# Sums of the inputs stored unsplit by GpSimd, split after reloading; the attention's memory pool on the other side; one difference on VectorE

## The chip, the cores and the metric

The kernel runs on one core of one Trainium2 chip. The metric is the device time of one execution in microseconds (us). The engines that matter here are TensorE (PE, matrix multiplications), VectorE (DVE), ScalarE (ACT), GpSimd (POOL) and SyncE (SP). SP does nothing but issue transfers (DMAs), one after the other, in a fixed order; GpSimd has a queue of transfers of its own. All transfers of both queues share the core's 16 DMA engines.

## The reference

One step of a one-layer streaming encoder, for 512 new frames and 32 frames of a running stream, which the kernel treats as one block of T = 544 columns. Cut to what this case touches:

```
h   = layer_norm(x)                                  # 2048 features per frame
proj = h @ w_in                                      # split into hq, hf, hi, hg (8 heads each), cq, ckv, kr
o_h = hgrn2(hq, 1-f, log f, hi, state)               # gated linear recurrence, head by head
q   = rms_norm(cq) @ w_q_b ;  lat = rms_norm(ckv)    # latent attention, 8 heads
k, v = (lat_past ++ lat) @ w_kv_b
o_a = softmax(q k^T + q_rope k_rope^T, chunk mask) v
out = concat(o_h, o_a) @ w_out
h   = layer_norm(ALPHA * h + out)
y   = layer_norm(ALPHA * h + conv_ffn(h))
```

Everything is float32. The outputs are y, the new latents and rope keys, the recurrent states and the last rows of the convolution.

## The kernel before, in words

**Tiles.** Activations lie transposed: 128 features on the partitions, T = 544 columns. `h` is 16 such tiles (k = 0..15), kept as a high and a low half (`aH`, `aL`) so that a float32 product is three passes of TensorE: high by high, low by high weight, high by low weight (`mm3`, L148). `H_` are the two halves of the columns, 272 each. A weight block of 128x1024 is loaded into `raw` (`load_raw`, L127), split into `wh` by ACT (L136) and `wl` by DVE (L137). The unsplit tiles of `h` also lie in DRAM as `h0d`.

**Stages in order of time.** Layer norm of the input, transposes and the `cq` projection; then the attention stage, whose tiles come from the pool `mp` (and `mpr`): projections of `ckv` and `kr`, head 0's q and f (`head_qf(0)`), four pairs of attention heads (`proj_pair`, `attend`) and head 0's i and g (`head_ig(0)`), interleaved by `weave`. Then the divided products for heads 1 to 7 with pools `smr` and `gp`; then the first output piece (`out_first`); then the output projection, the norm and the feed-forward part.

**Divided products.** For heads 1 to 7 a product of 1024 inputs by 2 is made as seven products of half size instead of eight (`divided`, in the order 11, s1, s2, s4, s3, 12, 22; 24 multiplications of 272 columns each, L865). They need four signed sums of the half rows of tile k and tile 8+k, for k = 0..7: s1, s2, s3, s4.

**The sums, before.** `sums_of_inputs` makes them beside the `ckv`, `kr` and `head_qf(0)` products. For each k it loads two rows of `h0d` (L685, L686, 272 KB each, on SP), combines their halves with four DVE operations of 272 columns (L183, L186), splits both results into high (ACT, L697) and low (DVE, L698), and stores the halves with four transfers on SP (L700, 272 KB each). The tiles for the rows are reused (three `p`, two `kn`), and so are the four that hold the split results, so that later loads and splits wait for earlier stores. Later s1 and s2 (L730) come back as already split tiles of 1088 KB, s3 into the freed column halves of `aH` and `aL` (L765), and s4 (L730) into pool `gp`.

**What sets the order.** Each engine runs its instructions in the order in which they were put; SP's list is one queue, so a transfer that waits for something holds all transfers behind it, weights included. `form_next` puts copies of w_out blocks (`wf...`, L93) on SP and accumulating ones on GpSimd at set places. In the divided stage PE, DVE and ACT follow an order written by hand: `turns` says at which slot (half a product) the steps of `levels` (the recurrence's tables, L904 to L946) and `finish` of a head run. `levels(0)` begins at slot 0, before the s1 product.

**The end of the attention stage.** `attend(3)` stores its outputs `o` (`catd`, L670), GpSimd takes the difference of its two heads in place (L671), and SP stores it (`d3d`, L672). The pools of the divided stage overlay the memory of `mp`: `Kp` (L907) lies where `o` lay, so it waits for that last store.

**After the divided stage.** `out_first` multiplies cat tiles, reloaded into `cx` (slots of the old s1, s2 tiles) and split. The next stage loads `h0d` rows into `za` (GpSimd, L1505) and `zb`, adds the output, and takes column sums (L1127). `za` overlays tiles that the last `finish` still stores from (`sm`).

Of the kernel before, what the change touches and what calls it, by code (L numbers as in the profile page):

```python
# [7 lines left out]
F32 = mybir.dt.float32  # L8
# [51 lines left out]
def tile_encoder_step(ctx, tc, xp, xs, w_in, w_in4, w_kr, w_q_b, w_kv_b, w_out, w_out4, w_up, w_gate, w_down, w_down2,  # L60
# [16 lines left out]
    d3_dr = [dram.tile([P, 2, NI], F32, name=f"d3d{k}", tag=f"d3d{k}") for k in range(HK // 2)]  # L77
    si_dr = {n: [dram.tile([P, 2, 4, NI], F32, name=f"si{n}{i}", tag=f"si{n}{i}") for i in range(2)]
             for n in ("s1", "s2", "s3", "s4")}
    sm_dr = [dram.tile([P, 3, 4, NI], F32, name=f"sm{i}", tag=f"sm{i}") for i in range(2)]  # L80
# [320 lines left out]

    with tc.tile_pool(name="mp", bufs=1) as mp, tc.tile_pool(name="psa", bufs=4, space=PSUM) as psa:
        mpr_stack = ExitStack()
        mpr = mpr_stack.enter_context(tc.tile_pool(name="mpr", bufs=1, side="right", reuse_waits="tile"))
        cos = mpr.tile([P, T], F32, name="cos")
# [205 lines left out]
        def attend(pr):  # L611
# [17 lines left out]
            def turn(b, p):  # L629
                tp = a_tile()  # L630
                t = mp.tile([P, 512], F32, name="pT", tag="pT", bufs=3)
                if b == 4:
                    PE.transpose(tp[:, 0:P], p[:, 0:P], ident)
                    PE.transpose(tp[:, P:2 * P], p[:, 32:160], ident)
                    A.activation(plast[96:128, :], tp[96:128, P:P + 64], AF.Copy)
                    n = 64
                else:
                    n = (b + 1) * P
                    for k in range(b + 1):
                        PE.transpose(tp[:, k * P:(k + 1) * P], p[:, k * P:(k + 1) * P], ident)  # L640
                A.activation(t[:, :n], tp[:, :n], AF.Copy)
                return t
# [27 lines left out]
            dma(cat_dr[4 + pr], o)  # L670
            G.tensor_tensor(out=o[:, :, :NI], in0=o[:, :, :NI], in1=o[:, :, NI:], op=ALU.subtract)  # L671
            dma(d3_dr[pr], o[:, :, :NI])  # L672
# [7 lines left out]

        def sums_of_inputs():
            for k in range(HK):
                tag, n, bufs = (("p", T, 3), ("kn", NK, 2))[k % 2]
                a, b = (mp.tile([P, n], F32, name=tag, tag=tag, bufs=bufs)[:, :T] for _ in range(2))
                dma(a, h0_dr[k])  # L685
                dma(b, h0_dr[HK + k])  # L686
                t0, t1, t0b, t1b = (x[:, h] for x in (a, b) for h in H_)
                yield
                minus(t1b, t1b, t1)
                minus(t1, t0, t1)  # L690
                opposite(t0, t1b, t0)
                opposite(t0b, t0, t0b)
                for x, names, (tag, n) in ((a, ("s2", "s3"), (("o", 2 * T), ("qr0", 2 * T))[k % 2]),
                                           (b, ("s4", "s1"), (("vt", 12 * P), ("qr1", 2 * T))[k % 2])):
                    hl = mp.tile([P, n], R, name=tag, tag=tag)[:, :2 * T].rearrange("p (i w c) -> p i w c", i=2, w=2)
                    x2 = x.rearrange("p (w c) -> p w c", w=2)
                    A.activation(hl[:, 0], x2, AF.Copy)  # L697
                    V.tensor_tensor(out=hl[:, 1], in0=x2, in1=hl[:, 0].bitcast(F32), op=ALU.subtract)  # L698
                    for w, name in enumerate(names):
                        dma(si_dr[name][k // 4][:, :, k % 4], hl[:, :, w].bitcast(F32))  # L700
                yield
# [11 lines left out]
        while len(forms) > 24:  # L713
            form_next()
        ropes = [[t[:, j * T:j * T + TP] for j in range(2)]
                 for t in (mp.tile([P, 2 * T], R, name=f"qr{g}", tag=f"qr{g}") for g in range(2))]
        run(proj_pair(0))
# [4 lines left out]
        sr_stack = ExitStack()  # L722
        smr = sr_stack.enter_context(tc.tile_pool(name="smr", bufs=1, side="right", reuse_waits="tile"))
        sums = {}

        def load_sum(p, name):
            sums[name] = [p.tile([P, 8 * NI], R, name=f"{name}{i}", tag=f"{name}{i}").rearrange("p (i k c) -> p i k c", i=2, k=4)
                          for i in range(2)]
            for i in range(2):
                dma(sums[name][i].bitcast(F32), si_dr[name][i])  # L730

        for name in ("s1", "s2"):
            load_sum(smr, name)
        weave([head_ig(0)], [attend(3)], 2.0)

# [12 lines left out]

    with tc.tile_pool(name="gp", bufs=1) as gp, tc.tile_pool(name="psg", bufs=1, space=PSUM) as psg:
        hm = gp.tile([P, T + 272 * 6], U8, name="hm")  # L750
# [11 lines left out]
        def place_s3():  # L762
            for k in range(HK):
                for i, t in enumerate((aH, aL)):
                    dma(t[k][:, H_[1]].bitcast(F32), si_dr["s3"][k // 4][:, i, k % 4])  # L765

# [270 lines left out]
        for n in range(2):  # L1037
            begin(n)
            complete(n)
        load_sum(gp, "s4")  # L1040
        place_s3()
        banks = [main_tile() for i in range(2)]
        last_finish = finish(HEADS - 1)
        with tc.manual_schedule(engines=MANUAL):
# [6 lines left out]

            beside_from(0, levels(0), (0, 1, 3, 4, 6, 8, 9, 11, 12))
            beside_from(15, finish(0), range(15))
# [16 lines left out]
        def out_first():  # L1070
            def split_cats(kk):
                cx = smr.tile([P, 4 * T], F32, name="cx", tag=("s10", "s11", "s20", "s10")[kk]).rearrange("p (k c) -> p k c", k=4)
                for i, k in enumerate(CAT_ORDER[4 * kk:4 * kk + 4]):
# [1583 lines left out]
```

## Time and profile before

| | |
|---|---|
| time, median of 3 runs | 2367.7 us (2366.69 to 2368.53) |
| the profiled execution | 2369.9 us, of which the span shown by the profile is 2368.1 |
| TensorE, matmuls | 2297.0 us busy, 97% of the span |
| VectorE | 1725.8 us, 73% |
| ScalarE | 1102.3 us, 47% |
| GpSimd | 274.7 us, 12% |
| bytes moved | 490 MB, mean 207 GB/s |

All numbers of the trace come from one profiled execution, and times within it are counted from the start of its span. A row that shows one instruction gives its start, its duration, the engine ("SPq" and "POOLq" are the issuing of transfers), the line and the operands, output first; in square brackets stands how long the engine was idle before it and what ended that. A row of the view by stretches gives for each engine its busy time and number of instructions, then the clock that TensorE was granted as a share of full speed ("PEclk"), the share of the DMA engines that was busy, and the GB/s. In the chain of waits each row is start, duration and what ran; "issue" is time with no visible cause.

### The profile page before, as it was taken

To read this page: it belongs to the slowest core of one execution; us is meant where nothing else is said; L and a number is where in the kernel's file an instruction comes from. 1 tells how busy PE (TensorE), PEld (TensorE's weight loads), DVE (VectorE), ACT (ScalarE), POOL (GpSimd) and SP (SyncE) were. 2 spreads that over 40 slices of the span, in tenths; PEclk is the share of its full clock that TensorE was granted. 3 is DMA by queue.
4 is the path that set the end of the run, shared out by engine and by line. 5 is a ranking of instruction groups with operands and counts; after the bars stand their busy time and mean duration, and the time that the engine had idled before them with its cause. 6 is when DMAs were issued, how large, how long until landed. Compare 5 with 4: busy or idle time off the path is not lost.

```text
span 2368.1 us, 44628 instructions
## 1 busy us (share of the span) xinstructions
PE 2297.0 (97%) x18210; PEld 2280.2 (96%) x18210; DVE 1725.8 (73%) x2393; ACT 1102.3 (47%) x1686; POOL 274.7 (12%) x339
## 2 busy tenths in 40 slices
PE   7969989999998999999999999999999999999997
PEld 7969989999998999999999999999999999999997
DVE  7646646777776778988777777777777777777776
ACT  6335423444433545765555555555555433333324
POOL 1001101111100221101000010000100111111102
PEclk9989989999999999999999999999999999999998
DMA  7762466767666764677766767667676999889842
GB/s 253 243 219 82 151 180 147 182 163 171 170 160 227 258 202 164 192 211 206 213 198 179 227 165 223 190 184 223 166 226 187 359 329 295 258 284 306 296 107 78
DMA packets 182460, 490.02 MB, mean 207 GB/s; under 512 B 16368, under 2 KB 84720, under 8 KB 174064
## 3 DMA queue, kind: packets, MB, share of 16 engines
q1 hardware_dynamic: 146480, 334.13, 40.5%
q0 software_dynamic: 35776, 153.04, 28.1%
q8 instruction: 143, 2.34, 0.4%
q14 instruction: 61, 0.50, 0.1%
HBM read 403.14 MB, written 98.03 MB: 212 GB/s over the span
## 4 chain that ended last, share of the span: by engine, by line
PE 90%; DMA 3%; DVE 3%; ACT 2%; issue 1%; SPq 1%; POOL 0%; ACTq 0%; DVEq 0%; POOLq 0%
PE main L1319 22%; PE acc L1319 17%; PE main L865 12%; PE main L1350 10%; PE main L148 8%; PE acc L1350 7%; PE acc L148 3%; PE s L930 2%; PE main L1804 1%; PE sb L1804 1%; PE main L593 1%; PE at L654 1%; PE at L623 1%; DMA xr<-wf1s 1%; DMA raw<-in_w_in 1%
## 5 line engine op out<-in xcount | busy, mean ns | idle before, releaser
L1261 DVE TENSOR_TENSOR wl<-raw,wh 128x1024 fp32r<-128x1024 f32 x371 | 456.0, 1229 | 194.8 <-ACT wh L1260 194.6
L1260 ACT ACTIVATE wh<-raw 128x1024 fp32r<-128x1024 f32 x371 | 392.5, 1059 | 410.4 <-PE main L1319 100.8
L1319 PE MATMUL main<-op,wh 128*128 128x272 f32 x1408 | 265.4, 287 | 0.0
L1319 PE MATMUL acc<-ops,wh 128*128 128x272 f32 x1344 | 254.1, 287 | 0.0
L1319 PE MATMUL main<-ops,wh 128*128 128x272 f32 x1344 | 254.1, 287 | 0.0
L1319 PEld LDWEIGHTS main<-op,wh 128*128 128x128 f32 x1408 | 221.0, 188 | 0.0
L1319 PEld LDWEIGHTS acc<-ops,wh 128*128 128x128 f32 x1344 | 211.1, 188 | 0.0
L1319 PEld LDWEIGHTS main<-ops,wh 128*128 128x128 f32 x1344 | 211.0, 188 | 0.0
L1319 PE MATMUL main<-op,wl 128*128 128x272 f32 x704 | 202.9, 288 | 0.3 <-DVE wl L1261 0.3
L1319 PE MATMUL main<-ops,wl 128*128 128x272 f32 x672 | 193.7, 288 | 0.0
L1319 PE MATMUL acc<-ops,wl 128*128 128x272 f32 x672 | 193.7, 288 | 0.0
L1319 PE MATMUL acc<-op,wh 128*128 128x272 f32 x832 | 157.5, 288 | 1.0 <-ACT ea L1645 1.0
L1260 ACT ACTIVATE wh<-rawl 128x1024 fp32r<-128x1024 f32 x93 | 98.8, 1063 | 117.4 <-PE acc L1319 45.8
L807 DVE TENSOR_TENSOR wl<-raw,wh 128x1024 fp32r<-128x1024 f32 x98 | 120.3, 1228 | 43.6 <-ACT wh L802 42.5
L148 PE MATMUL main<-aH,wh 128*128 128x272 f32 (+2 forms) x480 | 122.5, 298 | 19.6 <-ACT wh L136 19.4
L865 PE MATMUL main<-s,wh 128*128 128x272 f32 x672 | 133.7, 296 | 0.0
L1261 DVE TENSOR_TENSOR wl<-rawl,wh 128x1024 fp32r<-128x1024 f32 x93 | 113.8, 1223 | 27.0 <-ACT wh L1260 26.9
L865 PE MATMUL main<-aH,wh 128*128 128x272 f32 x448 | 133.2, 297 | 0.0
L1319 PEld LDWEIGHTS main<-op,wl 128*128 128x128 f32 x704 | 132.2, 188 | 0.5 <-DVE wl L1261 0.5
L802 ACT ACTIVATE wh<-raw 128x1024 fp32r<-128x1024 f32 x98 | 103.3, 1055 | 62.5 <-DVE raw L794 58.0
L1319 PEld LDWEIGHTS acc<-op,wh 128*128 128x128 f32 x832 | 130.4, 188 | 1.2 <-ACT ea L1645 1.2
L865 PE MATMUL main<-aH,wl 128*128 128x272 f32 x448 | 129.6, 289 | 0.0
(518 smaller groups left out, 6189.8 us busy)
## 6 DMA issues: line engine op xcount, KB each, us to landing
raw<-in_w_in SPq DMA_DIRECT2D x76, 512.0 KB, 5.2
raw<-in_w_up SPq DMA_DIRECT2D x71, 512.0 KB, 5.2
raw<-in_w_gate SPq DMA_DIRECT2D x71, 512.0 KB, 4.7
raw<-in_w_down SPq DMA_DIRECT2D x67, 512.0 KB, 9.1
opd<-ohl SPq DMA_DIRECT2D x20, 1088.0 KB, 5.5
ops<-opd POOLq DMA_DIRECT2D x20, 1088.0 KB, 11.8
raw<-in_w_up POOLq DMA_DIRECT2D x35, 512.0 KB, 5.2
opd<-ohl SPq DMA_DIRECT2D x20, 816.0 KB, 6.5
```

The lines of the kernel that those rows point to most:

```text
L148: PE.matmul(ps, ww[:, wcols[0]:wcols[1]], aa[:, hs[j]], start=first and i == 0, stop=last and i == 2, skip_group_check=True)
L593: PE.matmul(ps[:, j * 512:j * 512 + 256], l[k][:, a:b], r4(w[:, k:k + 1, :])[:, 0, :, 128:256], start=k == 0 and i == 0, stop=k == 1 and i ...
L623: PE.matmul(sc[:, :nk], qn[j][:, q0:q0 + P], kn[j][:, :nk], start=True, stop=False)
L802: A.activation(wh, self.t(self.key), AF.Copy)
L807: V.tensor_tensor(out=wl, in0=self.t(self.key), in1=wh.bitcast(F32), op=ALU.subtract)
L865: PE.matmul(out, ww[:, k * P:(k + 1) * P], aa, start=name in ("11", "s1", "12") and k == 0 and q == 0, stop=k == HK - 1 and q == 2, skip_g ...
L930: PE.matmul(ps[:, j * 64:(j + 1) * 64], Kp[:, a:b], Qv[:, j * bt:(j + 1) * bt, 1, :], start=True, stop=True)
L1260: A.activation(wh, src, AF.Copy)
L1261: V.tensor_tensor(out=wl, in0=src, in1=wh.bitcast(F32), op=ALU.subtract)
L1319: PE.matmul(ps, ww[:, k * P:(k + 1) * P], aa, start=self.first and k == 0 and i == 0, stop=k == n - 1 and i == 2, skip_group_check=True)
L1350: PE.matmul(banks[:, 512 * u:512 * u + NI], ww[:, (u * n + k) * P:(u * n + k + 1) * P], aa, start=self.first and k == 0 and i == 0, stop=k ...
L1804: PE.matmul(self.bank, ww[:, k * P:(k + 1) * P], aa, start=self.first and k == 0 and i == 0, stop=k == HK - 1 and i == 2, skip_group_check ...
```

## The change

1. `sums_of_inputs` first loads all 16 rows (L696), each into a tile of its own (three `p`, two `kn`, three `pT`, two each in `o`, `vt`, `qr0`, `qr1`; `pT` is widened from 512 to 544 columns for it). Then come all 32 combinations on DVE. The results are not split: GpSimd stores them raw, 16 transfers of 272 KB (L707).
2. The sums are loaded raw (L738, 544 KB a tile; s3 into the `aL` halves only, L781) and split by ACT and DVE afterwards: s1 and s2 during `attend(3)` (L742, L743, 1088 columns), s4 and s3 at set slots within the first divided product, s3 in 8 pieces of 272 columns (L787). `levels(0)` begins at slot 2 instead of 0, so the s1 product runs before it.
3. `mp` now lies on the right side of the memory and `mpr` on the left, `smr` on the left and `gp` on the right, the last two and `mp` with waits by tile. The loads of s4 and the fourth raw slot (`raw21`) are the first tiles of `gp`. `za` (L1535 now) thereby lies over `raw21`'s place.
4. The last pair's difference of heads (L671) runs on DVE; the other three stay on GpSimd.
5. `cx` takes the tiles of s2, s2, s1, s1 in turn, instead of s1, s1, s2, s1.

```diff
@@ -75,8 +75,8 @@
     d3_dr = [dram.tile([P, 2, NI], F32, name=f"d3d{k}", tag=f"d3d{k}") for k in range(HK // 2)]
-    si_dr = {n: [dram.tile([P, 2, 4, NI], F32, name=f"si{n}{i}", tag=f"si{n}{i}") for i in range(2)]
-             for n in ("s1", "s2", "s3", "s4")}
+    si_dr = {n: [dram.tile([P, 4, 2, NI], F32, name=f"si{n}{i}", tag=f"si{n}{i}") for i in range(2)] for n in ("a", "b")}
+    SI = {"s2": ("a", 0), "s3": ("a", 1), "s4": ("b", 0), "s1": ("b", 1)}
     sm_dr = [dram.tile([P, 3, 4, NI], F32, name=f"sm{i}", tag=f"sm{i}") for i in range(2)]
@@ -399,9 +399,9 @@
 
-    with tc.tile_pool(name="mp", bufs=1) as mp, tc.tile_pool(name="psa", bufs=4, space=PSUM) as psa:
+    with tc.tile_pool(name="mp", bufs=1, side="right", reuse_waits="tile") as mp, tc.tile_pool(name="psa", bufs=4, space=PSUM) as psa:
         mpr_stack = ExitStack()
-        mpr = mpr_stack.enter_context(tc.tile_pool(name="mpr", bufs=1, side="right", reuse_waits="tile"))
+        mpr = mpr_stack.enter_context(tc.tile_pool(name="mpr", bufs=1))
         cos = mpr.tile([P, T], F32, name="cos")
@@ -628,7 +628,7 @@
                 tp = a_tile()
-                t = mp.tile([P, 512], F32, name="pT", tag="pT", bufs=3)
+                t = mp.tile([P, T], F32, name="pT", tag="pT", bufs=3)
                 if b == 4:
@@ -668,7 +668,7 @@
             dma(cat_dr[4 + pr], o)
-            G.tensor_tensor(out=o[:, :, :NI], in0=o[:, :, :NI], in1=o[:, :, NI:], op=ALU.subtract)
+            (V if pr == 3 else G).tensor_tensor(out=o[:, :, :NI], in0=o[:, :, :NI], in1=o[:, :, NI:], op=ALU.subtract)
             dma(d3_dr[pr], o[:, :, :NI])
@@ -679,25 +679,32 @@
         def sums_of_inputs():
+            homes = [("p", T, 3)] * 3 + [("kn", NK, 2)] * 2 + [("pT", T, 3)] * 3
+            homes += [(t, n, 1) for t, n in (("o", 2 * T), ("vt", 12 * P), ("qr0", 2 * T), ("qr1", 2 * T))]
+
+            def room():
+                for tag, n, bufs in homes:
+                    t = mp.tile([P, n], F32, name=tag, tag=tag, bufs=bufs)
+                    for i in range(n // T):
+                        yield t[:, i * T:(i + 1) * T]
+
+            rooms = room()
+            rows = []
             for k in range(HK):
-                tag, n, bufs = (("p", T, 3), ("kn", NK, 2))[k % 2]
-                a, b = (mp.tile([P, n], F32, name=tag, tag=tag, bufs=bufs)[:, :T] for _ in range(2))
-                dma(a, h0_dr[k])
-                dma(b, h0_dr[HK + k])
+                rows.append((next(rooms), next(rooms)))
+                for x, kg in zip(rows[k], (k, HK + k)):
+                    dma(x, h0_dr[kg])
+                if k % 2:
+                    yield
+            for k in range(HK):
+                a, b = rows[k]
                 t0, t1, t0b, t1b = (x[:, h] for x in (a, b) for h in H_)
-                yield
                 minus(t1b, t1b, t1)
                 minus(t1, t0, t1)
                 opposite(t0, t1b, t0)
                 opposite(t0b, t0, t0b)
-                for x, names, (tag, n) in ((a, ("s2", "s3"), (("o", 2 * T), ("qr0", 2 * T))[k % 2]),
-                                           (b, ("s4", "s1"), (("vt", 12 * P), ("qr1", 2 * T))[k % 2])):
-                    hl = mp.tile([P, n], R, name=tag, tag=tag)[:, :2 * T].rearrange("p (i w c) -> p i w c", i=2, w=2)
-                    x2 = x.rearrange("p (w c) -> p w c", w=2)
-                    A.activation(hl[:, 0], x2, AF.Copy)
-                    V.tensor_tensor(out=hl[:, 1], in0=x2, in1=hl[:, 0].bitcast(F32), op=ALU.subtract)
-                    for w, name in enumerate(names):
-                        dma(si_dr[name][k // 4][:, :, k % 4], hl[:, :, w].bitcast(F32))
+                for x, n in ((a, "a"), (b, "b")):
+                    G.dma_start(si_dr[n][k // 4][:, k % 4], x.rearrange("p (w c) -> p w c", w=2))
                 yield
@@ -713,24 +720,32 @@
         ropes = [[t[:, j * T:j * T + TP] for j in range(2)]
-                 for t in (mp.tile([P, 2 * T], R, name=f"qr{g}", tag=f"qr{g}") for g in range(2))]
+                 for t in (mp.tile([P, 2 * T], R, name=f"qr{g}", tag=f"qr{g}", bufs=1) for g in range(2))]
         run(proj_pair(0))
         weave([proj_pair(1)], [attend(0)], 2.0)
         weave([proj_pair(2)], [attend(1)], 2.0)
         weave([proj_pair(3)], [attend(2)], 2.0)
         mpr_stack.close()
         sr_stack = ExitStack()
-        smr = sr_stack.enter_context(tc.tile_pool(name="smr", bufs=1, side="right", reuse_waits="tile"))
+        smr = sr_stack.enter_context(tc.tile_pool(name="smr", bufs=1, reuse_waits="tile"))
         sums = {}
 
         def load_sum(p, name):
             sums[name] = [p.tile([P, 8 * NI], R, name=f"{name}{i}", tag=f"{name}{i}").rearrange("p (i k c) -> p i k c", i=2, k=4)
                           for i in range(2)]
             for i in range(2):
-                dma(sums[name][i].bitcast(F32), si_dr[name][i])
+                ab, w = SI[name]
+                dma(sums[name][i][:, 1].bitcast(F32), si_dr[ab][i][:, :, w])
+
+        def split_sum(name, i):
+            h, l = (sums[name][i][:, n] for n in range(2))
+            A.activation(h, l.bitcast(F32), AF.Copy)
+            V.tensor_tensor(out=l, in0=l.bitcast(F32), in1=h.bitcast(F32), op=ALU.subtract)
 
         for name in ("s1", "s2"):
             load_sum(smr, name)
+            for i in range(2):
+                split_sum(name, i)
         weave([head_ig(0)], [attend(3)], 2.0)
@@ -746,7 +761,9 @@
 
-    with tc.tile_pool(name="gp", bufs=1) as gp, tc.tile_pool(name="psg", bufs=1, space=PSUM) as psg:
+    with tc.tile_pool(name="gp", bufs=1, side="right", reuse_waits="tile") as gp, tc.tile_pool(name="psg", bufs=1, space=PSUM) as psg:
+        load_sum(gp, "s4")
+        raw21 = gp.tile([P, HK * P], F32, name="raw21", tag="raw21", bufs=1)
         hm = gp.tile([P, T + 272 * 6], U8, name="hm")
@@ -761,8 +778,15 @@
             for k in range(HK):
-                for i, t in enumerate((aH, aL)):
-                    dma(t[k][:, H_[1]].bitcast(F32), si_dr["s3"][k // 4][:, i, k % 4])
+                dma(aL[k][:, H_[1]].bitcast(F32), si_dr["a"][k // 4][:, k % 4, 1])
+
+        def split_s3(ks):
+            for k in ks:
+                h, l = aH[k][:, H_[1]], aL[k][:, H_[1]]
+                A.activation(h, l.bitcast(F32), AF.Copy)
+                V.tensor_tensor(out=l, in0=l.bitcast(F32), in1=h.bitcast(F32), op=ALU.subtract)
+                if k % 2:
+                    yield
 
@@ -1037,7 +1061,6 @@
             complete(n)
-        load_sum(gp, "s4")
         place_s3()
@@ -1049,7 +1072,14 @@
 
-            beside_from(0, levels(0), (0, 1, 3, 4, 6, 8, 9, 11, 12))
+            def split_s4():
+                for i in range(2):
+                    split_sum("s4", i)
+                    yield
+
+            beside_from(1, split_s4(), (0, 2))
+            beside_from(4, split_s3(range(HK)), range(4))
+            beside_from(0, levels(0), (2, 3, 5, 6, 7, 8, 9, 11, 12))
             beside_from(15, finish(0), range(15))
@@ -1069,7 +1099,7 @@
             def split_cats(kk):
-                cx = smr.tile([P, 4 * T], F32, name="cx", tag=("s10", "s11", "s20", "s10")[kk]).rearrange("p (k c) -> p k c", k=4)
+                cx = smr.tile([P, 4 * T], F32, name="cx", tag=("s20", "s21", "s11", "s10")[kk]).rearrange("p (k c) -> p k c", k=4)
                 for i, k in enumerate(CAT_ORDER[4 * kk:4 * kk + 4]):
                     if k != HEADS - 1:
                         dma(cx[:, i], cat_dr[k // 2][:, k % 2, :])
```

How the order of instructions changes is shown at three places. The first is SP's queue where the weights of `head_qf(0)` are loaded, in four pieces 0 to 3 of 48 multiplications each; `raw<-in_w_in` at the end is piece 2. In the kernel before (`t`, `lx` and `out_lat` belong to the rope and the latents):

```order
L685 DMA p<-h0d_75 128x544
L686 DMA p<-h0d_83 128x544
L685 DMA kn<-h0d_76 128x544
L686 DMA kn<-h0d_84 128x544
L93 DMA wf3s_117<-in_w_out 16x8192
...
L494 DMA lx<-in_latp 128x128
...
L700 DMA sis_100<-qr_1628 256x1x272
L700 DMA sis_102<-qr_1628 256x1x272
L700 DMA sis_104<-qr_1633 256x1x272
L700 DMA sis_98<-qr_1633 256x1x272
L127 DMA raw<-in_w_in 128x1024
```

and the same place now, from the last loads of rows on:

```order
L696 DMA qr_1157<-h0d_75 128x544
L696 DMA qr_1157<-h0d_83 128x544
L696 DMA qr_1160<-h0d_76 128x544
L696 DMA qr_1160<-h0d_84 128x544
L127 DMA raw<-in_w_in 128x1024
L93 DMA wf3s_113<-in_w_out 16x8192
L494 DMA lx<-in_latp 128x128
L127 DMA raw<-in_w_in 128x1024 x2
L93 DMA wf4s_117<-in_w_out 16x8192
```

The three `raw<-in_w_in` rows are pieces 1, 2 and 3; they stand directly behind the 16 loads of rows, and no store of a sum is left on SP.

The second is GpSimd's queue in the same stretch. `r` is the power that the norm of `ckv` needs (L447), the first one the norm of `cq`. Before:

```order
L417 MEMSET ql_971 128x384
L418 MEMSET plast 128x64
L447 TENSOR_TENSOR r_1030<-r_1029,nhalf 128x5
L447 TENSOR_TENSOR r_1491<-r_1490,nhalf 128x5
L464 TENSOR_TENSOR t<-t,cos 128x544
```

and now:

```order
L447 TENSOR_TENSOR r_1030<-r_1029,nhalf 128x5
L707 DMA sia_97<-p 128x544
L707 DMA sib_99<-p 128x544
...
L707 DMA sia_98<-qr_1160 128x544
L707 DMA sib_100<-qr_1160 128x544
L447 TENSOR_TENSOR r_1451<-r_1450,nhalf 128x5
L464 TENSOR_TENSOR t<-t,cos 128x544
```

All 16 stores stand between the two powers, ahead of the one for `ckv`.

The third is DVE where the attention stage ends (`o` is the last attention output, `hproj` head 0's gate, `s_3572` and `s_3573` the two tiles of s4). Before:

```order
L651 COPY o<-at 128x2x32
L398 TENSOR_TENSOR hproj<-hproj,main 128x544
L907 TENSOR_SCALAR Kp<-hproj 128x544
L908 TENSOR_TENSOR Qp<-hproj 128x544
L914 COPY_PREDICATED attnT_3638<-hm,sw 128x544
L934 TENSOR_TENSOR Qp<-Qp,hproj 128x272
```

and now:

```order
L651 COPY o<-at 128x2x32
L671 TENSOR_TENSOR o<-o 128x2x272
L398 TENSOR_TENSOR hproj<-hproj,main 128x544
L743 TENSOR_TENSOR s_3572<-s_3572 128x1088
L831 TENSOR_TENSOR wl<-raw,wh 128x1024
L931 TENSOR_SCALAR Kp<-hproj 128x544
L932 TENSOR_TENSOR Qp<-hproj 128x544
L743 TENSOR_TENSOR s_3573<-s_3573 128x1088
L938 COPY_PREDICATED attnT_3579<-hm,sw 128x544
```

The difference L671, the split of s4's first tile and a split of weights now stand ahead of `Kp`, on which the first table product (`sw<-hproj,Kp`, L913 before, L937 now) depends.

## The prediction

> **What bounds the kernel now.** I read the page first. TensorE (PE) is busy 97% of the span and carries nine tenths of the chain of waits, so other engines matter only where PE stands.
>
> ```profile
> PE 2297.0 (97%) x18210; PEld 2280.2 (96%) x18210; DVE 1725.8 (73%) x2393; ACT 1102.3 (47%) x1686; POOL 274.7 (12%) x339
> PE 90%; DMA 3%; DVE 3%; ACT 2%; issue 1%; SPq 1%; POOL 0%; ACTq 0%; DVEq 0%; POOLq 0%
> ```
>
> PE's waits between 78 and 830 us by line, and the view by stretches, place three holes that the change touches, one at each of the first three rows:
>
> ```profile
> PE main L148 <- ACT wh L136: 19.4, 1, 19.4
> PE sw L913 <- DVE Kp L907: 7.4, 2, 7.2
> PE sb L1127 <- DVE n_e L1138: 6.3, 1, 6.3
> 78.00:120.00 42.00, 41.80 (x337) 41.61 (x336) 33.64 (x64) 15.78 (x25) 3.35 (x5) 1.00 0.81 267
> 120.00:146.00 26.00, 7.15 (x59) 6.93 (x57) 12.28 (x24) 5.13 (x8) 1.88 (x1) 0.70 0.88 283
> 152.00:320.00 168.00, 166.35 (x1237) 157.07 (x1236) 93.31 (x259) 83.93 (x186) 19.80 (x26) 1.00 0.42 128
> 340.00:360.00 20.00, 20.00 (x167) 19.78 (x167) 15.73 (x33) 5.99 (x10) 0.90 (x1) 1.00 0.35 101
> 735.00:760.00 25.00, 25.00 (x206) 24.94 (x205) 14.01 (x24) 7.34 (x8) 1.71 (x2) 1.00 0.47 151
> ```
>
> Between the holes PE is nearly full at clock 1.00, so nothing is gained there, only lost.
>
> **Part 1, the stores leave SP: hole 1.** SP's first load of a row; the chain of waits behind the 19.4 us; then PE's rows around it:
>
> ```profile
> 79.97 0.59 SPq L685 DMA_DIRECT2D p<-h0d  x1
> 138.65 0.57 SPq L700
> ...
> 141.28 4.12 DMA raw<-in_w_in
> 145.43 1.06 ACT wh L136
> 146.54 0.82 PE L148 MATMUL main<-aH,wh 128*128 128x272 f32 x2 [19.39 <-ACT wh L136]
> ...
> 151.10 0.41 PE L148 MATMUL main<-aH,wh 128*128 128x272 f32 x2
> 151.35 0.41 PE L148 MATMUL main<-aL,wh 128*128 128x272 f32 x2
> ```
>
> The load that PE needed, piece 2 of `head_qf(0)`, took 4.12 us, but was issued only at 141.28, behind the last four stores. From 151.10 on a pair starts every 0.25 us, 0.126 for one; the 19 multiplications from 146.54 to 151.10 took 4.56 us where 2.4 would do: 2.2 lost to a lowered clock. Hole 1 costs 19.4 + 2.2 = 21.6 us.
>
> With the change no store is ahead of that load, only the 16 loads of rows. These are 16 x 0.279 = 4.5 MB, at 267 GB/s 17 us; issued from 80 us, they are in by about 97, and pieces 1 to 3, at 4 to 5 us each, by about 112. PE wants piece 2 at 146.54 - 19.39 = 127.15.
>
> What is late next? DVE makes all 32 combinations before it splits piece 0, and a piece is 48 x 0.126 = 6.0 us, so that split is wanted at 127.15 - 12 = 115. These two kinds of DVE instruction between 78 and 150 us price it:
>
> ```profile
> L698 DVE TENSOR_TENSOR qr<-kn,qr 128x544 fp32r<-128x544 f32 x8 | 5.6, 719 | 0.3 <-ACT qr L697 0.3
> L183 DVE TENSOR_TENSOR p<-p 128x272 f32<-128x272 f32 x8 | 3.5, 439 | 1.8 <-DMA p<-h0d 1.6
> ```
>
> From 78 to 120 DVE worked 33.64 us. Twelve splits (8.6) go from that stretch, eight combinations (3.5) come into it: 28.5, over at 107 if it never waits, and its loads are in by 97. Margin 8 us. So I count part 1 in full: -21.6, and at worst -16.5 (rival A).
>
> By the Trainium skill ("DMA: Bandwidth & Descriptors", Rules for kernel authors), spreading transfers over SP, ACT and GpSimd brings no bandwidth, since all share the same 16 DMA engines; it saves only issuing time on the queue. That speaks against the change if the hole is one of bandwidth, and from 120 to 146 the DMA engines are 0.88 busy; by the rule the sum would end where rival A does.
>
> **Part 2, the sums are split later.** Four splits of 1088 columns (s1, s2) fall into the last attention pair: by the prices above, 4 x 1.1 us of ACT and 4 x 1.4 of DVE. Between 152 and 320 us DVE is busy 93.31 of 168 us, ACT 83.93: they fit, unless one stands at its engine before its load has landed, 0 to 3 us. Two of s4 and eight of s3 come into the first divided product: 2 x 1.4 + 8 x 0.44 = 6.3 us of DVE in some 30 us, where 340 to 360 has it 15.73 of 20 busy and thus 6.4 free in 30. That just fits on average; 0 to 3 us may come through. Together +2 (0 to +6). The new tiles for `cx` I count at nothing: at 735 to 760 PE has 25.00 of 25 us of work while they load and are split. Without that cover a late tile costs PE its whole load of 4 to 5 us, which the 6 includes.
>
> **Parts 3 and 4, the end of attention: hole 2.** The chain of waits from the last store of `o`, and two groups of transfers with KB and median us to landing:
>
> ```profile
> 315.81 7.88 DMA catd<-o
> ...
> 325.21 2.53 DMA d3d<-o
> ...
> 327.87 0.87 DVE Kp L907
> ...
> 328.83 2.31 PE sw L913 x10
> ...
> 333.25 5.63 PE main L865 x24
> 338.88 0.84 PE s L930 x8
> catd<-o SPq DMA_DIRECT2D x4, 544.0 KB, 2.8
> p<-h0d SPq DMA_DIRECT2D x8, 272.0 KB, 4.4
> ```
>
> `Kp` no longer waits for `d3d`. But on SP s4's reload stands behind `d3d`, and on DVE `Kp` stands behind s4's first split. With `catd` as slow as here it lands at 323.7; the difference on DVE, 0.72, ends at 324.4; `d3d` and s4's first load are issued by 325.1; that load of 544 KB takes some 5.5 (between the 4.4 and the 7.88); then ACT 1.1, DVE 1.4, a split of weights 1.2 and `Kp` 0.9: 335.2. The two tables (333.25 - 328.83) end at 339.6. The s1 product runs in the gap before them. Today the same work is done at 338.88. One wait takes another's place: I value it at 0. If `catd` takes 2.8 instead of 7.88 it is -4.5; if s4's load takes 7.88 too and a little of the low clock comes on top, +3.
>
> **Part 3, the end of the divided stage: hole 3.** GpSimd's row, two pieces of the chain, and a stretch further on:
>
> ```profile
> 759.48 2.76 POOL L1505 DMA_DIRECT2D za<-h0d  x5 [11.10 <-PE main L148]
> 760.11 7.26 DMA za<-h0d
> 768.43 2.72 PE sb L1127 x12
> 771.15 5.20 PE sb L148 x24
> 795.00:805.00 10.00, 10.00 (x81) 10.00 (x81) 8.53 (x11) 6.73 (x8) 2.46 (x2) 1.00 1.03 408
> ```
>
> PE ended at 768.43 - 6.3 = 762.1 and stood until `za` had landed and been added. Now `za` lies over a raw slot that the last divided product frees before 735, where the output piece begins, so its 7.26 us are over long before 762. What stays is three operations of 272 columns and their hand-overs, about 1.6 us: 4.7 gained. The 24 multiplications took 5.20 instead of 3.0: 2.2 more at a full clock. That is 6.9, at most 8.3 if the 2.72 shrink by half. From 795 to 805 the DMA engines are full (1.03), and part of PE's lead waits for bytes there: I take -6 (0 to -8.3).
>
> **Sum.** -21.6 + 2 + 0 - 6 = -25.6. From the profiled execution's 2369.9 that is 2344.3; this lies 2.2 above the median of the runs, 2367.7, hence 2342.
>
> **Rivals.** (A) *Hole 1 is bandwidth.* From 80 to 141.28, 40 x 267 + 21.3 x 283 = 16.7 MB moved. If only the halved stores count, 4.5 MB less at 272 GB/s, the load goes out 16.5 us earlier, at 124.8, and PE starts at 130.0: a wait of 3 and a low clock of 2 stay, 2347. Against it: the load itself landed in 4.12. (B) *Hole 3 stays*, because the full DMA engines behind it (1.03) give the lead back: 2348. (C) *Slower: GpSimd's queue.* All 16 stores stand ahead of the power that the `ckv` norm needs; these are its row and another of that queue:
>
> ```profile
> 117.18 1.30 POOL L447 TENSOR_TENSOR r<-r,nhalf 128x5 f32<-128x5 f32 x1 [31.40 <-DVE r L446]
> 321.69 0.89 POOL L93 DMA_DIRECT2D wf1s<-in_w_out  x1 [8.17 <-issue]
> ```
>
> At `za`'s 2.76 / 5 = 0.55 us each the stores take 9 us, from about 88 on, and cost nothing. But the transfer at 321.69 stood 8.17 us in the queue. At 4.5 us a store the power would come at 88 + 72 = 160 instead of 118.5, PE would stand for up to 41 us, and the time would be 2383; it decides from a delay of 25.6 us, that is 3.5 us a store. (D) *It does not do what it says*: piece 2 is early on SP, but its slot comes free late, so that most of hole 1 stays and the rest of the sum brings 4: 2363. Against it: three slots take turns, and this one was read three pieces earlier.
>
> **How the numbers follow.** Forecast 0.63, A 0.10, B 0.17, C 0.05, D 0.05. A change of 0.2%, 4.7 us, is about what a measurement can tell from none. Forecast, A and B lie beyond it: faster 0.90; D lies on its edge: same 0.05; C: slower 0.05. Range: the best ends give -21.6 - 4.5 - 8.3 = -34.4, so 2333; upwards it holds A, B, and B with most of part 2's 6 on top: 2355.
>
> **What would show it.** Right: before 150 us no wait of PE at L148 over 3 us and a clock of 1.00; the raw loads of `head_qf(0)` issued before 115; at `sw` still 5 to 12 us of waiting, now behind s4's split; at L1127 under 2 us, with `za` issued before 755. Wrong: a wait at the `ckv` norm's matrix rows (C), at piece 0 near 115, over 5 us of new waits in the first divided product, or one behind 785.

## The result, and the profile after

The changed kernel takes 2342.06 us (2341.88 to 2343.88, 4 runs) against 2367.19 (2366.47 to 2368.53, 4 runs): a ratio of 0.9895, 95% interval 0.9878 to 0.9912. In a later comparison on another occasion it was 0.9889 (0.9874 to 0.9903). The forecast was 2342. Its profiled execution has a span of 2340.1, 28.0 less than the 2368.1 before; the median of the runs fell by 25.1. The terms below are read from the two profiled executions, so they add up to 28.0.

The page of the changed kernel, and the waits of PE between 60 and 830 us that are read below:

```profile
PE 2293.4 (98%) x18210; PEld 2276.8 (97%) x18210; DVE 1724.8 (74%) x2392; ACT 1099.5 (47%) x1684; POOL 280.6 (12%) x354
```

```profile
PE sw L937 <- DVE Kp L931: 5.5, 2, 5.4
PE main L889 <- DVE hproj L398: 2.5, 1, 2.5
PE at L640 <- DVE mx L605: 1.0, 1, 1.0
PE at L623 <- ACT p L606: 0.7, 1, 0.7
```

The waits of 19.4 at L148 and of 6.3 at the column sums are gone. At `sw` 5.4 of 7.2 is left; 2.5 stands new ahead of the s1 product, and 1.0 and 0.7 stand new in the last attention pair. The same stretches as before, and three others (PE busy first, then the other engines; the last three numbers are the clock, the DMA engines' busy share and GB/s):

```profile
78.00:120.00 42.00, 42.00 (x341) 42.00 (x340) 30.61 (x63) 11.30 (x17) 11.27 (x18) 1.00 0.90 330
120.00:146.00 26.00, 26.00 (x211) 26.00 (x210) 11.04 (x18) 8.79 (x15) 1.56 (x2) 1.00 0.45 136
318.00:323.00 5.00, 5.00 (x29) 5.00 (x30) 4.28 (x9) 0.19 (x1) 0.00 (x0) 0.66 0.14 32
358.00:363.00 5.00, 5.00 (x30) 5.00 (x30) 2.74 (x5) 0.00 (x0) 0.00 (x0) 0.66 0.72 128
735.00:749.00 14.00, 14.00 (x115) 13.94 (x114) 7.75 (x16) 2.78 (x3) 0.00 (x0) 1.00 0.93 323
```

From 78 to 146 us PE does not stand at all and has clock 1.00. To see where the time went, the same single multiplication of PE is looked up in both traces, and the start of its row is compared (the 338.88 of the chain of waits counts from the end of the row before):

| work that begins | before | after | difference | in this part |
|---|---|---|---|---|
| last multiplication ahead of the wait for piece 2 | 126.86 | 126.21 | -0.7 | -0.7, before that |
| the multiplication from which the clock was full again behind that wait | 151.10 | 128.71 | -22.4 | -21.7, hole 1 |
| last multiplication ahead of L623 in the last attention pair | 291.94 | 269.07 | -22.9 | -0.5, attention up to there |
| last multiplication of the first divided product (11) | 321.36 | 300.68 | -20.7 | +2.2, last attention pair |
| the next level or product once 11, s1 and the first two tables are done | 338.68 | 317.98 | -20.7 | 0.0, hole 2 |
| last multiplication of the output piece, before its column sums | 761.88 | 744.82 | -17.1 | +3.6, divided products |
| the multiplications behind the second sums (L1132, L1162) | 776.19 | 749.30 | -26.9 | -9.8, hole 3 |
| end of the span | 2368.1 | 2340.1 | -28.0 | -1.1 |

**Hole 1.** SP's weights for `head_qf(0)` (pieces 1, then 2 and 3), and the first and last raw store and the power for the `ckv` norm on GpSimd:

```profile
90.15 0.33 SPq L127 DMA_DIRECT2D raw<-in_w_in  x1
101.44 4.59 SPq L127 DMA_DIRECT2D raw<-in_w_in  x2
87.82 0.79 POOL L707 DMA_DIRECT2D sia<-p  x1 [2.61 <-DVE p L186]
105.83 0.54 POOL L707 DMA_DIRECT2D sib<-qr  x1
116.55 1.20 POOL L447 TENSOR_TENSOR r<-r,nhalf 128x5 f32<-128x5 f32 x1 [10.19 <-DVE r L446]
```

Piece 2 went out at 101.44 instead of 141.28, and the stores left GpSimd free 10 us before the power was wanted. The bytes that moved between 80 and 141 us, before and then after:

```profile
DMA packets 11953, 16.65 MB, mean 273 GB/s; under 512 B 1280, under 2 KB 9197, under 8 KB 11885
```

```profile
DMA packets 6757, 16.50 MB, mean 271 GB/s; under 512 B 1386, under 2 KB 1770, under 8 KB 6705
```

They are the same: where stores went, later weights now come. So the mean over these 61 us is the same too and says nothing of a limit; from 78 to 120 us the rate rose from 267 to 330 GB/s. The Trainium skill ("DMA: Bandwidth & Descriptors", Rules for kernel authors) says that spreading transfers over queues brings no bandwidth. This change cannot test it, since it also makes the stores fewer and their rows longer; `e2_gp_only` below, which moves the stores alone, has 263 GB/s from 78 to 120 us and 323 from 120 to 146, against 267 and 283 before, which does not settle it. That the hole was the order, and not the bandwidth, is for the experiments to show.

**The last attention pair.** The splits of s1 and s2, on ACT and on DVE, and PE's two new waits:

```profile
266.50 1.11 ACT L742 ACTIVATE s<-s 128x1088 fp32r<-128x1088 f32 x1 [2.87 <-DMA s<-sia]
268.47 1.09 ACT L742 ACTIVATE s<-s 128x1088 fp32r<-128x1088 f32 x1
270.12 1.28 DVE L743 TENSOR_TENSOR s<-s 128x1088 fp32r<-128x1088 f32 x1
270.06 0.91 PE L623 MATMUL at<-kn,t 128*128 128x384 f32 x2 [0.71 <-ACT p L606]
272.34 0.41 PE L640 MATMUL at<-ident,p 128*128 128x128 f32 x2 [1.01 <-DVE mx L605]
```

ACT stood 2.87 us at a split until its load had landed. Behind that came a split of weights and the other split of s2, and only then, at 269.47, the exponentials `p` (L606), which PE waited for at L623. On DVE the last split stood ahead of the operations that PE waited for at L640. Part 2 of the change costs 2.2 us here. The kernel before and `e2_gp_only`, which have no such splits, have neither wait; every other run below has both.

**Hole 2.** From several engines, in order of time: the difference on DVE, SP's loads of s4, its first split on ACT and on DVE, `Kp`, and PE:

```profile
302.09 0.73 DVE L671 TENSOR_TENSOR o<-o 128x544 f32<-128x544 f32 x1 [6.99 <-DMA catd<-o]
303.52 1.27 SPq L738 DMA_DIRECT2D s<-sib  x2
309.71 1.11 ACT L742 ACTIVATE s<-s 128x1088 fp32r<-128x1088 f32 x1 [11.11 <-DMA s<-sib]
310.85 1.29 DVE L743 TENSOR_TENSOR s<-s 128x1088 fp32r<-128x1088 f32 x1 [7.40 <-ACT s L742]
313.19 0.44 DVE L931 TENSOR_SCALAR Kp<-hproj 128x544 f32<-128x544 f32 x1
313.69 2.34 PE L937 MATMUL sw<-hproj,Kp 128*128 128x128 f32 x10 [5.38 <-DVE Kp L931]
317.98 0.80 PE L889 MATMUL main<-s,wh 128*128 128x272 f32 x2
```

`Kp` stands behind s4's split, s4's load behind the difference, and this behind `catd`, which took from 295.14 to about 302.

**Hole 3.** `za` on GpSimd, the last operation ahead of the column sums on DVE, and PE:

```profile
731.01 2.77 POOL L1535 DMA_DIRECT2D za<-h0d  x5
743.76 0.44 DVE L1168 TENSOR_TENSOR n_e<-za 128x272 f32<-128x272 f32 x1
744.94 1.39 PE L1157 MATMUL sb<-ones,n_e 128*128 128x1 f32 x12
746.20 0.37 PE L148 MATMUL sb<-aH,wh 128*128 128x272 f32 x1
```

PE goes from the output piece into the sums without a wait.

### The profile page after: what moved, and what is told of

Same layout as the page of the kernel before. It is cut to its first block, busy times and chain, and to the rows that moved or that the text cites. A ratio compares the mean times of both kernels' runs of the same rounds, so it can differ in the third digit from the quotient of the medians.

```text
span 2340.1 us, 44591 instructions
## 1 busy us (share of the span) xinstructions
PE 2293.4 (98%) x18210; PEld 2276.8 (97%) x18210; DVE 1724.8 (74%) x2392; ACT 1099.5 (47%) x1684; POOL 280.6 (12%) x354
## 4 chain that ended last, share of the span: by engine, by line
PE 64%; ACT 1%; DVE 1%; issue 0%; ACTq 0%; DVEq 0%
PE main L1349 22%; PE acc L1349 17%; PE main L1380 11%; PE acc L1380 7%; PE acc L148 3%; PE main L148 1%; PE main L1834 1%; PE sb L1834 1%; ACT y L2435 0%; ACT wh L1290 0%; PE main L1162 0%; ACT zb L1490 0%; PE main L1157 0%; ACT za L1490 0%; PE acc L1157 0%
## 5 line engine op out<-in xcount | busy, mean ns | idle before, releaser
L889 PE MATMUL main<-aL,wh 128*128 128x272 f32 x448 | 129.0, 288 | 0.0
```

The lines of the kernel that those rows point to most:

```text
L889: PE.matmul(out, ww[:, k * P:(k + 1) * P], aa, start=name in ("11", "s1", "12") and k == 0 and q == 0, stop=k == HK - 1 and q == 2, skip_g ...
```

## The experiments

All ratios are to the kernel before, on the same chip and in the same rounds, with 95% intervals; beside them stand the changed kernel's 0.9895 and 0.9889.

### What made hole 1: the queue, the reuse of tiles, or the bytes

**Stores back on SP** (`e1_sp_stores`).

```diff
-                    G.dma_start(si_dr[n][k // 4][:, k % 4], x.rearrange("p (w c) -> p w c", w=2))
+                    dma(si_dr[n][k // 4][:, k % 4], x.rearrange("p (w c) -> p w c", w=2))
```

> The change with its 16 raw stores issued by SP instead of GpSimd; the early loads with a place for every row, and half the bytes, stay. If the hole was SP's order (theory), SP now holds 16 stores, and behind them the copies for the rope, ahead of piece 1, so piece 1 cannot be issued before about 120 and piece 2 before about 125: PE waits again at L148, 8 to 20 us in all, and the time is 2352 to 2364. If it was bytes, or the tiles that were reused (rivals), nothing comes back: 2342 +- 2.

Measured: 2349.66 us, ratio 0.9919 (0.9904 to 0.9934). PE's waits at L148, and SP's piece 2:

```profile
PE main L148 <- ACT wh L136: 3.6, 1, 3.6
PE main L148 <- DVE wl L137: 0.9, 1, 0.9
```

```profile
126.05 0.44 SPq L127 DMA_DIRECT2D raw<-in_w_in  x1
```

The theory's time for piece 2 was right (126), but PE waited only 4.5 us, less than the 8 to 20 expected, and the time lies below the range. With places for all rows, 16 stores on SP delay the weights by 25 us and still cost only some 6 us.

**Only the queue** (`e2_gp_only`): the kernel before, its 32 stores issued by GpSimd.

```diff
-                        dma(si_dr[name][k // 4][:, :, k % 4], hl[:, :, w].bitcast(F32))
+                        G.dma_start(si_dr[name][k // 4][:, :, k % 4], hl[:, :, w].bitcast(F32))
```

> The kernel before, with its 32 stores of split sums issued by GpSimd and nothing else changed: rows still share tiles, bytes are as before. SP's order theory: piece 2 stands on SP behind the loads of row 5 only, is issued by about 115 to 122, and the 19.4 us wait at L148 is gone; a few us may come at the ckv norm, since 24 stores stand ahead of its power; time 2345 to 2354. Bytes rival: hole 1 stays at 15 us or more, 2362 or above. Reuse rival: row loads wait for slower stores, piece 2 comes after 127, 2355 to 2365.

Measured: 2363.94 us, ratio 0.9978 (0.9969 to 0.9988). PE's waits in that stretch, then a split and the evacuation behind it on ACT, SP's piece 2 and the power on GpSimd:

```profile
PE main L148 <- ACT t L520: 6.8, 1, 6.8
PE at L452 <- POOL r L447: 5.4, 1, 5.4
```

```profile
122.79 0.66 ACT L697 ACTIVATE qr<-kn 128x544 fp32r<-128x544 f32 x1 [4.14 <-DMA sis<-qr]
123.36 0.60 ACT L520 ACTIVATE t<-main 128x544 f32<-128x544 f32 x1
113.51 0.45 SPq L127 DMA_DIRECT2D raw<-in_w_in  x1
135.99 1.32 POOL L447 TENSOR_TENSOR r<-r,nhalf 128x5 f32<-128x5 f32 x1
```

Each theory is half right. Piece 2 goes out at 113.51 and the 19.4 us wait for weights is gone, at full bytes. But two new waits take most of the gain: ACT holds an evacuation (`t`, L520) behind a split whose tile waits for a store to land, and 24 stores stand ahead of the power, which comes at 135.99 instead of 117.18. That is the forecast's rival C in kind. The reuse of tiles shows in ACT's wait, but what spaces the stores out is the queue itself. From the fourth of them on, each of these 24 stores of 256 rows was issued 0.31 us after the one three places ahead had landed (the fourth at 97.23, the first having landed at 96.91; the 24th at 135.40, the 21st having landed at 135.09): never more than three were under way.

**Twice the stores** (`e6_double`): each raw store is issued a second time, into a buffer that nothing reads.

```diff
+    sj_dr = {n: [dram.tile([P, 4, 2, NI], F32, name=f"sj{n}{i}", tag=f"sj{n}{i}") for i in range(2)] for n in ("a", "b")}
...
-                    G.dma_start(si_dr[n][k // 4][:, k % 4], x.rearrange("p (w c) -> p w c", w=2))
+                    for d in (si_dr, sj_dr):
+                        G.dma_start(d[n][k // 4][:, k % 4], x.rearrange("p (w c) -> p w c", w=2))
```

> The change with each raw store issued twice by GpSimd, the second time into a buffer that nothing reads: as many bytes stored as before the change, and 32 transfers on GpSimd's queue. If bytes made hole 1 (rival), PE waits at L148 again, 3 us or more. If it was SP's order (theory), there is no wait at L148. GpSimd's queue: 32 x 0.6 us from 88 on, with eight in flight at a time, make the ckv norm's power come at 116 to 135, so a wait of 0 to 12 us at the norm's matrix rows: 2342 to 2356.

Measured: 2348.94 us, ratio 0.9912 (0.9897 to 0.9927). No wait at L148; the one new wait ahead of 290 us, and the power:

```profile
PE at L453 <- POOL r L448: 3.5, 1, 3.5
```

```profile
124.65 1.21 POOL L448 TENSOR_TENSOR r<-r,nhalf 128x5 f32<-128x5 f32 x1
```

With the old number of bytes stored, PE does not wait for weights, and from 78 to 120 us the DMA engines move 372 GB/s. Rival A falls. What it does meet is GpSimd's queue: 32 stores end at 124.6 after 87.8, 1.15 us each, and the norm waits 3.5 us. The expectation counted on eight under way at a time; of these stores of 128 rows there were never more than seven, the eighth being issued at 94.83, after the first had landed at 94.52. So the change's margin on that queue was real but not wide.

Together: the 19.4 us wait came from SP's order. The other queue alone (`e2_gp_only`) removes it and brings two others; a place for each row and 16 raw stores, left on SP (`e1_sp_stores`), leave 4.5 us of it; the change, with all of these, leaves none there. Which of the places, the smaller number of stores and their fewer rows spares it the new waits of `e2_gp_only` was not run apart; the number alone is worth the 3.5 us of `e6_double`.

### What made hole 3

**Pools back on their old sides** (`e5_sides`). Of each line only the call is shown.

```diff
-tc.tile_pool(name="mp", bufs=1, side="right", reuse_waits="tile")
+tc.tile_pool(name="mp", bufs=1)
-tc.tile_pool(name="mpr", bufs=1)
+tc.tile_pool(name="mpr", bufs=1, side="right", reuse_waits="tile")
-tc.tile_pool(name="smr", bufs=1, reuse_waits="tile")
+tc.tile_pool(name="smr", bufs=1, side="right", reuse_waits="tile")
-tc.tile_pool(name="gp", bufs=1, side="right", reuse_waits="tile")
+tc.tile_pool(name="gp", bufs=1)
```

> The change with the four pools back on their old sides and with their old waits; loads, stores, splits and the rest stay as in the change. If za's place made hole 3 (theory), za is issued at its old point, after the last sums are stored, and PE waits about 6 us at L1157 again with a low clock behind it, +8 to +10; at the first divided product Kp lies over o again and waits for the store of d3d, which s4's split waits for longer, so 0 to +2 there: 2350 to 2354. Rival: the early za is due to the work behind being earlier or to the cx tiles, and hole 3 stays away: 2341 to 2345.

Measured: 2355.0 us, ratio 0.9942 (0.9926 to 0.9959), 11 to 12.5 us more than the changed kernel. GpSimd's `za`, PE's column sums, and SP's load of s4:

```profile
745.34 2.77 POOL L1535 DMA_DIRECT2D za<-h0d  x5 [11.40 <-PE main L148]
754.59 2.72 PE L1157 MATMUL sb<-ones,n_e 128*128 128x1 f32 x12 [6.59 <-DVE n_e L1168]
309.16 1.20 SPq L738 DMA_DIRECT2D s<-sib  x2
```

Hole 3 is back as it was: `za` at 745 rather than 731, a wait of 6.59, and 2.72 for the sums instead of 1.39. Of the 12.4 us between the two profiles 9.4 come there. The layout of the pools made it; their sides and their waits went back together, so that it is the place of `za` and not the waits is argued, not shown. At hole 2 it costs another 3.5 us: s4's load goes out at 309.16 instead of 303.52, since on that side it too waits for `d3d` to land (3.3 us on SP).

**Old tiles for `cx`** (`e11_cx_old`). Of the line only the tags are shown.

```diff
-tag=("s20", "s21", "s11", "s10")[kk]
+tag=("s10", "s11", "s20", "s10")[kk]
```

> The change with the old tiles for cx (s1, s1, s2, s1), all else as in the change. Theory: the tiles of cx neither cost nor brought anything, since PE is full while they load: within 1 us of the change. Rival: part of hole 3's gain, which was larger than forecast, comes from them: 2 to 4 us slower than the change, with a wait at L1157 or within the output piece.

Measured: 2342.98 us, ratio 0.9887 (0.9872 to 0.9901), beside 2343.21 for the changed kernel in the same rounds. Part 5 of the change neither costs nor brings anything that can be measured.

### What is left in hole 2

**The last difference back on GpSimd** (`e4_diff_pool`).

```diff
-            (V if pr == 3 else G).tensor_tensor(out=o[:, :, :NI], in0=o[:, :, :NI], in1=o[:, :, NI:], op=ALU.subtract)
+            G.tensor_tensor(out=o[:, :, :NI], in0=o[:, :, :NI], in1=o[:, :, NI:], op=ALU.subtract)
```

> The change with the last pair's difference L671 back on GpSimd, all else as in the change. Theory: hole 2 is set by s4's reload, which waits on SP behind d3d; the slower difference (1.33 instead of 0.72) makes it some 0.8 later, while L398 no longer stands behind the difference on DVE, so the 2.5 us wait ahead of the s1 product goes and is only found again at sw: 2342 to 2344. Rival: the difference on DVE is worth more, as GpSimd also issues other transfers there and blocks: 2346 or above.

Measured: 2344.42 us, ratio 0.9897 (0.988 to 0.9913). PE's first waits:

```profile
PE sw L937 <- DVE Kp L931: 11.1, 2, 11.0
```

The 2.5 us wait at L398 is gone and `sw` waits 11.0 instead of 5.4. Part 4 alone is worth nothing that can be measured: it hurries `d3d` and holds the s1 product.

**s4's splits two slots later** (`e3_s4_later`).

```diff
-            beside_from(1, split_s4(), (0, 2))
+            beside_from(3, split_s4(), (0, 2))
```

> The change with the two splits of s4 moved from slots 1 and 3 to slots 3 and 5 of the first divided product, so that Kp stands ahead of them on DVE. If hole 2 is now the reload of s4 through DVE's order (theory), the 5.4 us wait at sw goes to under 1, and with it 0 to 3 us of low clock: 2334 to 2337. Rival: another wait takes its place (s4's product waits for its tiles, or the tables' data are late anyway): 2341 to 2343.

Measured: 2340.5 us, ratio 0.9881 (0.9866 to 0.9895). PE's waits:

```profile
PE main L889 <- DVE hproj L398: 4.8, 1, 4.8
PE s L954 <- DVE Kp L960: 2.6, 1, 2.6
```

The wait at `sw` is gone, which shows that it was DVE's order. Less than the 5 to 8 us expected is won, and by the intervals the time cannot be told from the changed kernel's: L398 still stands behind the difference and so behind `catd`, and the next table's data behind s4's split.

**Off that chain altogether** (`e7_last_off_sp`): difference on GpSimd, its store on GpSimd's queue, splits later.

```diff
-            (V if pr == 3 else G).tensor_tensor(out=o[:, :, :NI], in0=o[:, :, :NI], in1=o[:, :, NI:], op=ALU.subtract)
-            dma(d3_dr[pr], o[:, :, :NI])
+            G.tensor_tensor(out=o[:, :, :NI], in0=o[:, :, :NI], in1=o[:, :, NI:], op=ALU.subtract)
+            (G.dma_start if pr == 3 else dma)(d3_dr[pr], o[:, :, :NI])
-            beside_from(1, split_s4(), (0, 2))
+            beside_from(3, split_s4(), (0, 2))
```

> The change with three edits at the end of attention: the last difference on GpSimd, its store d3d on GpSimd's queue instead of SP's, and s4's splits at slots 3 and 5. Theory: then neither L398 nor Kp nor s4's load waits for the slow store catd; the waits ahead of the s1 product (2.5) and at sw (5.4) both go, and the low clock with them (3): 2331 to 2334. Rival: a data wait a little further on (s4's product or the tables) takes most of it back: 2337 to 2341.

Measured: 2337.8 us (2336.35 to 2338.3), ratio 0.9865 (0.9851 to 0.988). All its runs lie below all of the changed kernel's, which ran at other times. PE's first wait, and what DVE's tables waited for:

```profile
PE s L954 <- DVE Kp L960: 5.1, 2, 3.1
```

```profile
312.09 0.76 DVE L938 COPY_PREDICATED attnT<-hm,sw 128x544 f32<-128x544 uint8 x1 [2.13 <-DMA hm<-in_hmask]
```

Both waits are gone, but 5.1 us come back at the next tables, whose mask `hm` was loaded last. The time lies in the rival's range, and so does the cause: a wait for data a little further on.

**Later still, and the mask first** (`e8_last_off_sp_later`, `e9_mask_first`, `e10_mask_first_later`). The first has s4's splits at slots 4 and 5; the second is `e7_last_off_sp` with the mask loaded ahead of s4 (`fetch_sum` issues s4's two loads); the third has both.

```diff
-            beside_from(3, split_s4(), (0, 2))
+            beside_from(4, split_s4(), (0, 1))
```

```diff
-        load_sum(gp, "s4")
+        load_sum(gp, "s4", False)
...
         dma(hm, hmask_d)
+        fetch_sum("s4")
```

> As e7, with s4's splits at slots 4 and 5 instead of 3 and 5, so that the first tables' data are made ahead of them on DVE. Theory: 0 to 2 us better than e7, since no DVE operation of the tables stands behind s4's load: 2330 to 2333. Rival: s4's product now waits for the split: 1 to 3 us worse than e7.

> The version with the last difference, its store and s4's splits moved (s4 split at slots 3 and 5), with the mask hm, which the tables need on DVE and which landed at 311.8 there, now issued ahead of s4's two loads. Theory: the mask lands some 4 us earlier, and the 3.1 us wait at the second table falls to what s4's own landing leaves, 1 to 2: ratio to the kernel before lower by 0 to 0.1%, about 0.986. Rival: s4 lands later by as much and takes the gain back: 0.9865 or above.

> The same with s4's splits at slots 4 and 5. Theory: now neither the mask nor s4 stands ahead of the first tables on DVE, their waits go from 4.1 to under 1.5 us, and with them most of the 8 us of low clock: ratio 0.983 to 0.985. Rival: s4's product waits for the late split: 0.986 to 0.988.

Measured: 2340.22 us, ratio 0.9878 (0.9864 to 0.9893); 2339.69, 0.9871 (0.9854 to 0.9887); 2339.52, 0.9872 (0.9857 to 0.9886). None beats `e7_last_off_sp`. By the intervals the four cannot be told apart, but each run of the first, taken side by side with `e7_last_off_sp`, was slower than each of that one. In the second the wait at the table grew to 4.7, since s4 now landed later. In the third, PE's waits moved to s4's product:

```profile
312.50 0.39 PE L895 MATMUL main<-s,wh 128*128 128x272 f32 x1 [0.99 <-ACT s L747]
315.42 0.60 PE L895 MATMUL main<-s,wh 128*128 128x272 f32 x1 [2.53 <-DVE s L748]
```

So the times are those of the rivals in all three, and in the second and third their causes too. From 300 to 310 us the DMA engines are nearly full here too:

```profile
300.00:310.00 10.00, 9.35 (x77) 9.16 (x76) 3.54 (x7) 2.79 (x5) 4.20 (x6) 1.00 0.95 253
```

`catd`, accumulating transfers, a weight, the mask and s4 all fall into it, and putting one first makes another late.

**The change once more** (`e12_change_again`), the kernel itself in the rounds of the last three.

> The changed kernel itself, on the same chip and in the same rounds as the three others, so that they can be compared with it directly: 2341 to 2344, ratio 0.989 to 0.990. Every theory expects the same of it; should the granted clock not fall behind the two small waits near 350 us this time, it is up to 1.7 faster.

Measured: 2343.21 us, ratio 0.9889 (0.9874 to 0.9903), as all expected. Against it `e10_mask_first_later` is 3.7 us faster in the same rounds.

## Why the prediction was right, point by point

- **Part 1 (-21.6): -21.7.** Cause, place and size were as worked out: the rows were in, DVE had made its combinations by 106, and piece 2 was issued 26 us before it was wanted. Another 1.2 us were gained ahead of hole 1 and in attention, which the forecast does not have.
- **Part 2 (+2, 0 to +6): +2.2 at the splits of s1 and s2, and +3.6 in the divided products by another road.** For the last attention pair the forecast set 0 to 3, "unless one stands at its engine before its load has landed": that is what ACT did, for 2.87 us. For the divided products it set 0 to 3 for DVE's extra work. Between hole 2 and the output piece PE's waits are the same four as before (1.3, 0.8, 0.8, 0.2), so that work was hidden. What was lost is clock: 0.66 from 318 to 323 and again from 358 to 363, each at most 5 x 0.34 = 1.7 us. The first belongs to hole 2. The second came in one profile of this kernel and not in the other, so about 1.6 of the 3.6 is chance.
- **Hole 2 (0): 0.0 up to 317.98, with the low clock behind it.** The step "one wait takes another's place" held in its details: the difference, s4's load, both halves of its first split and `Kp` follow in the order that was summed. `e3_s4_later` and `e4_diff_pool` show the two links of it.
- **Hole 3 (-6, at most -8.3): -9.8, beyond the bound.** The mechanism was right (`e5_sides`), a term was mis-sized. "What stays is three operations and their hand-overs, about 1.6 us" was wrong: the output piece ends with 24 multiplications that do not feed the sums, from 741.91 on, and DVE's operations, the last one at 743.76, run under them, so that the whole wait of 6.3 went. The `2.72` fell to 1.39, about as the bound had it. And nothing was lost to bytes behind 785: the rest of the way brought 1.1 more, 0.7 of it where a wait (L1804, now L1834) fell from 1.3 to 0.6.
- **The sum** came out at -25.6 against -28.0 between the two profiled executions and -25.1 between the medians. Too little gain was set at hole 3 (3.8), ahead of the last attention pair (1.3) and behind 785 (1.1), too little loss in part 2 (3.8); that these cancel to 2.4, and that the median lies within 0.1 us of the forecast, is luck. Rival A is refuted (`e6_double`), B and D by the trace; C did not happen, but `e6_double` shows that a queue twice as long is enough to bring on 3.5 us of it.

## What to carry to other kernels

On a queue that runs in order, ask of each urgent load what stands ahead of it and what that waits for; stores of results that are wanted late belong behind it or on another queue, their tiles should not be needed again soon, and one must look how many of them that queue has under way at a time. When a wait is removed, follow the chain of data past the next operation on the engine that feeds it: here `Kp` was freed of one store and put behind a load that stood in the queue behind the same store. Work moved into another stage, as the splits of s1 and s2 were, does harm where one of its operations stands at an engine before its data has landed, however idle that engine is on average. And what a wait really leaves is found only when one looks at which operations still run while the data arrives.

## What the runs showed of the hardware that was not expected

The granted clock costs as much as some of the waits, and not in proportion to them. After a wait, PE ran at about half speed (a multiplication every 0.227 instead of 0.126 us) for 4.6 us (hole 1, 146.54 to 151.10), 9.9 us (hole 2 before, 328.83 to 338.68), 7.8 us (hole 2 after, 313.69 to 321.48), 7.3 us (hole 3 before, 768.43 to 775.69) and 3.4 us (after the new wait of 2.5, 304.37 to 307.77). The Trainium skill ("TensorE: Matmul & The Clock Gate", Part 1) names at least one window of about 3.4 us of sustained work until full speed; the last of these stretches agrees, the others are longer. `e8_last_off_sp_later` waited less than `e7_last_off_sp` at the tables (4.1 against 5.1 us) and was not faster; its stretches from 310 on and those of `e7_last_off_sp` behind them:

```profile
310.00:320.00 10.00, 5.68 (x28) 5.15 (x28) 7.04 (x12) 5.31 (x10) 0.00 (x0) 0.74 0.60 217
320.00:330.00 10.00, 9.46 (x43) 9.16 (x43) 7.20 (x20) 0.06 (x1) 0.00 (x0) 0.50 0.17 54
```

```profile
310.00:320.00 10.00, 4.88 (x27) 4.37 (x25) 7.13 (x15) 5.72 (x12) 0.00 (x0) 0.83 0.59 163
320.00:330.00 10.00, 10.00 (x72) 10.00 (x73) 8.21 (x20) 2.00 (x3) 0.00 (x0) 0.83 0.24 64
```

At 0.50 against 0.83 over 10 us it gave back, by estimate, 3.3 us. And the same two small waits (0.8 and 1.3, some 8 us apart) were followed by a low clock in the first profile of the change (358 to 363: 0.66) and in that of `e9_mask_first` (355 to 360: 0.68), but not before the change nor in its second profile. Why is open; some 1.6 us of a comparison here can be that alone.

GpSimd's queue had at most seven stores of 128 rows under way (`e6_double`), and at most three of 256 rows (`e2_gp_only`). What sets these numbers is open.
